# First layer's down projection: later sums, eight block pairs in the last group, blocks from place 2

## The chip, the core and the metric

The kernel runs on one core of one Trainium2 chip. The metric is the device time of one execution in microseconds (us): 2175.49 us is the median of three runs before the change, which lay between 2175.35 and 2177.54 us. One further execution was profiled; all rows below come from it.

## What is computed

The reference is a trunk of two layers over 256 tokens with width 2048. Every layer adds a mixer (attention and a state-space part in the first, dilated attention in the second) and then a gated feed-forward network, and a norm ends the whole:

```python
for layer in range(DEPTH):                       # DEPTH = 2
    hn = rms_norm(h, mix_norm_w[layer])
    mix = even_mixer(hn, ...) if layer % 2 == 0 else odd_mixer(hn, ...)
    h = h + mix
    f = conv_ffn(rms_norm(h, ffn_norm_w[layer]), ..., w_down[layer])
    h = h + f
return rms_norm(h, final_norm_w)

def conv_ffn(hn, w_gate, w_up, conv_w, conv_b, w_down):
    g = causal_dwconv(hn @ w_gate, conv_w, conv_b)
    return (silu(g) * (hn @ w_up)) @ w_down      # the last product: 256 x 5632 by 5632 x 2048
```

The change concerns the last product of the first layer, `@ w_down`, and the first chunks of the odd mixer that follow it.

## The kernel before

**Products in two parts.** All is float32. The kernel splits each operand into a high part (a rounded copy, type fp32r) and a low part (the rest), and multiplies high by high, high by low and low by high: three terms (`TERMS`). A weight chunk arrives by one DMA of 512 KB into a `raw` buffer (four of them); ScalarE (ACT) rounds it to the high part in an `hl` buffer (three of them), L167; VectorE (DVE) subtracts to get the low part, L168. The activations were split before; they are the stationary operand in the down projection, and the weights stream.

**The down projection (`fold`).** It makes four groups of 512 output columns. A group runs over 22 chunks, each a pair of 128-row weight tiles by 512 columns; a chunk is at a place from 0 to 21 in the order `seq`. In group 0 a chunk is multiplied plainly by `whole` (L527, 512 columns each). In groups 1 to 3 a chunk goes one of two ways:

- *flat* (`flat` and `halves`, L575 and L578): the weight split of 1024 columns, then 24 matmuls of 256 columns;
- *block* (`pair_prep` and `seven`, L542): the chunk is seen as a 2 by 2 matrix of blocks and multiplied in the manner of Strassen and Winograd with seven block products instead of eight, 21 matmuls of 256 columns. `pair_prep` needs sums of weight blocks and splits them too: DVE L500, L503, L504 (sums), L505, L508, L509 (low parts), ACT L496, L506, L507 (high parts). The matching sums of the activations are made once, in group 0, by `pair_sums` (`S`), for nine chunks (`SP7`), and are kept in 16 `x` tiles, and in lent corners for the ninth.

Flat chunks stand first, then block and flat in turn: blocks at the odd places 3 to 19, so places 0, 1, 2, 20 and 21 are flat twice or thrice in a row.

**Sums at the end.** Four of the seven block products stay in two PSUM banks of their own (`aux1`) over the whole group. After the last block chunk `gather` turns them into the four column blocks' shares (ACT L611, DVE L612 to L616, "block sums"). After the last chunk `unfold` adds the group's PSUM rows (DVE L622, "row sums"; in group 0 an ACT copy), transposes the result on TensorE (PE, L631), adds it to the residual `h` (DVE L635) and sums squares for the next norm (ACT L637, DVE L638). In the last group the sums lie in a borrowed `raw` buffer, and `scale` makes the split inputs of the next layer: ACT L605, DVE L606, one of each for every one of the 16 tiles of 128 rows. Twelve of these belong to finished groups and four wait for the last group. They write into the `x` tiles that the block sums of the activations held.

**Order.** Helpers that span several chunks are generators in the list `bg`; `tick`, called after each chunk, moves each one on to its next `yield`. The Python order is only a wish: a scheduler puts each engine's instructions into a fixed list, and `issue_after` ties one instruction behind another of the same engine in that list. `self.lo` is the DVE instruction that ends the latest weight split. ACT and DVE work through their lists in order, and so does SyncE (SP), which issues the weight DMAs.

**After the down projection.** `odd` begins with steps of 16 pairs of matmuls (L243) and, after every second step, a plain chunk of values (L527). `token_scale` waits a number of ticks, sums the squares (DVE L123, PE L335), takes the root (small DVE operations) and spreads the result (PE L343, ACT L347 into `rbc`), which is first needed when a head's queries are finished after step 6.

## Time and profile before

| what | value |
|---|---|
| median of three runs | 2175.49 us (2175.35 to 2177.54) |
| the profiled execution | 2174.72 us, its span 2172.9 us, granted TensorE clock 0.999 |
| PE, busy share of the span | 99% (2161.1 us) |
| DVE, busy share | 77% (1681.0 us) |
| ACT, busy share | 57% (1228.0 us) |
| down projection of layer 1: groups 1, 2, 3 begin at | 902.92, 960.79 and 1018.72 us |
| first matmul of the odd mixer | 1080.03 us |

The span is the time from the first to the last profiled instruction; 1.8 us of the execution lie around it. A row of the timeline gives start, duration and engine; when like instructions follow each other they are one row with their count (x24). Matmul durations overlap, so the pace of PE is read from the starts of rows, not from the durations. Behind a row, in square brackets, stands how long the engine had been idle and what released it.

### The profile page before, as it was taken

To read this page: it belongs to the slowest core of one execution; us is meant where nothing else is said; L and a number is where in the kernel's file an instruction comes from. 1 tells how busy PE (TensorE), PEld (TensorE's weight loads), DVE (VectorE), ACT (ScalarE), POOL (GpSimd) and SP (SyncE) were. 2 spreads that over 40 slices of the span, in tenths; PEclk is the share of its full clock that TensorE was granted. 3 is DMA by queue.
4 is the path that set the end of the run, shared out by engine and by line. 5 is a ranking of instruction groups with operands and counts; after the bars stand their busy time and mean duration, and the time that the engine had idled before them with its cause. 6 is when DMAs were issued, how large, how long until landed. Compare 5 with 4: busy or idle time off the path is not lost.

```text
span 2172.9 us, 35607 instructions
## 1 busy us (share of the span) xinstructions
PE 2161.1 (99%) x13720; PEld 1948.9 (90%) x13720; DVE 1681.0 (77%) x2717; ACT 1228.0 (57%) x1857; POOL 96.8 (4%) x107
## 2 busy tenths in 40 slices
PE   9999999999999999999999999999999999999998
PEld 8888888888888888899989999888888888888998
DVE  8788776766666668789889998767676767688997
ACT  7556554655555555555555665546555555555554
POOL 0000000101010100000000000000010101000000
PEclk9999999999999999999999999999999999999999
DMA  7654555556556565556555555555555656566664
GB/s 264 236 171 148 172 184 194 191 193 193 194 193 193 195 193 192 194 194 204 182 188 186 188 169 196 171 190 188 185 194 194 194 194 194 193 201 201 209 202 169
DMA packets 117722, 417.65 MB, mean 192 GB/s; under 512 B 13072, under 2 KB 15408, under 8 KB 117552
## 3 DMA queue, kind: packets, MB, share of 16 engines
q1 hardware_dynamic: 116352, 412.48, 57.9%
q8 instruction: 107, 1.75, 0.3%
q0 software_dynamic: 576, 2.10, 0.3%
q10 hardware_dynamic: 624, 0.81, 0.1%
q14 instruction: 63, 0.52, 0.1%
HBM read 413.22 MB, written 2.11 MB: 191 GB/s over the span
## 4 chain that ended last, share of the span: by engine, by line
PE 96%; DVE 3%; issue 0%; DMA 0%; ACT 0%; DVEq 0%; ACTq 0%
PE acc L243 68%; PE acc L578 8%; PE acc L527 6%; PE aux L542 4%; PE acc L542 4%; PE acc L253 1%; PE aux L527 1%; DVE hl L168 1%; PE acc L204 1%; PE acc L260 1%; PE acc L212 0%; PE aux L212 0%; PE aux L970 0%; PE aux L1002 0%; DVE hl L505 0%
## 5 line engine op out<-in xcount | busy, mean ns | idle before, releaser
L243 PE MATMUL acc<-x,hl 128*128 128x512 f32 (+1 forms) x7680 | 1325.9, 334 | 0.0
L243 PEld LDWEIGHTS acc<-x,hl 128*128 128x128 f32 x7680 | 1158.7, 188 | 149.9 <-issue 0.9
L168 DVE TENSOR_TENSOR hl<-raw,hl 128x1024 fp32r<-128x1024 f32 x686 | 839.4, 1224 | 410.1 <-ACT hl L167 404.2
L167 ACT CAST hl<-raw 128x1024 fp32r<-128x1024 f32 x686 | 720.2, 1050 | 620.1 <-PE acc L243 363.6
L578 PE MATMUL acc<-hl,act 128*128 128x256 f32 x1848 | 223.8, 277 | 2.1 <-DVE hl L168 1.6
L578 PEld LDWEIGHTS acc<-hl,act 128*128 128x128 f32 x1848 | 217.0, 188 | 3.5 <-DVE hl L168 2.3
L243 PE MATMUL acc<-o,hl 128*128 128x512 f32 (+1 forms) x1024 | 176.0, 333 | 0.0
L302 ACT COPY ev<-acc 128x256 f32<-128x256 f32 x242 | 90.0, 372 | 149.5 <-PE acc L243 147.5
L243 PEld LDWEIGHTS acc<-o,hl 128*128 128x128 f32 x1024 | 154.4, 188 | 19.9
L868 POOL TENSOR_TENSOR cv<-cv,rbc 128x256 f32<-128x256 f32 x88 | 93.7, 1083 | 852.7 <-ACT cv L867 852.7
L527 PE MATMUL acc<-hl,act 128*128 128x512 f32 x528 | 120.1, 389 | 0.0
L527 PEld LDWEIGHTS acc<-hl,act 128*128 128x128 f32 x528 | 99.0, 188 | 20.5
L303 DVE TENSOR_TENSOR ev<-acc,ev 128x256 f32<-128x256 f32 x242 | 101.3, 421 | 4.4 <-ACT ev L302 2.7
L506 ACT CAST ts<-tf 128x768 fp32r<-128x768 f32 x78 | 65.2, 836 | 49.1 <-DVE tf L503 48.9
L508 DVE TENSOR_TENSOR ts<-tf,ts 128x768 fp32r<-128x768 f32 x78 | 74.4, 954 | 1.8 <-ACT ts L506 1.8
L500 DVE TENSOR_TENSOR tf<-raw 128x512 f32<-128x512 f32 x78 | 53.9, 691 | 9.6 <-DMA raw<-in_wd 8.0
L496 ACT CAST hl<-raw 128x768 fp32r<-128x768 f32 x54 | 45.1, 835 | 23.6 <-PE acc L578 13.1
L542 PE MATMUL aux<-ts,x 128*128 128x256 f32 x414 | 55.7, 276 | 0.0
L542 PE MATMUL acc<-hl,act 128*128 128x256 f32 x324 | 54.3, 276 | 0.0
L505 DVE TENSOR_TENSOR hl<-raw,hl 128x768 fp32r<-128x768 f32 x54 | 51.5, 954 | 1.9 <-ACT hl L496 1.6
L542 PEld LDWEIGHTS aux<-ts,x 128*128 128x128 f32 x414 | 50.9, 188 | 0.0
L878 DVE TENSOR_TENSOR ev<-ev,cv 128x256 f32<-128x256 f32 x88 | 38.3, 437 | 10.3 <-POOL cv L868 1.6
(280 smaller groups left out, 1693.1 us busy)
## 6 DMA issues: line engine op xcount, KB each, us to landing
raw<-in_wg SPq DMA_DIRECT2D x176, 512.0 KB, 4.1
raw<-in_wu SPq DMA_DIRECT2D x176, 512.0 KB, 4.2
raw<-in_wd SPq DMA_DIRECT2D x176, 512.0 KB, 4.2
raw<-in_wev SPq DMA_DIRECT2D x76, 512.0 KB, 3.8
raw<-in_wod SPq DMA_DIRECT2D x64, 512.0 KB, 3.9
raw<-in_wevo SPq DMA_DIRECT2D x32, 512.0 KB, 3.6
raw<-in_wodv SPq DMA_DIRECT2D x32, 512.0 KB, 3.6
raw<-in_wodo SPq DMA_DIRECT2D x32, 512.0 KB, 3.7
```

The source lines that it names most:

```text
L167: nc.scalar.copy(hi, raw)
L168: self.lo = nc.vector.tensor_tensor(lo, raw, hi.bitcast(F32), ALU.subtract)
L243: self.mm = self.nc.tensor.matmul(accs[nt][:, :n], hl[w][:, k, nt * P : (nt + 1) * P], xs[k0 + k][:, :n], start=start and k == w == 0, sto ...
L302: nc.scalar.copy(t, acc[:, T:])
L303: nc.vector.tensor_tensor(t, acc[:, :T], t, ALU.add)
L500: v.tensor_tensor(two(blk(f123, 0, 2)), two(blk(raw, 1, 2)), blk(raw, 3).unsqueeze(1).broadcast_to([P, 2, T]), ALU.subtract)
L506: nc.scalar.copy(t123[0], f123)
L508: v.tensor_tensor(t123[1], f123, t123[0].bitcast(F32), ALU.subtract)
L527: self.nc.tensor.matmul(row.rearrange("p (j c) -> p j c", c=T), self.part(a[k], p, tt), self.both(hl, w, k), start=start and i == k == 0, ...
L542: self.nc.tensor.matmul(to, x[p], w[b][q], start=n == 0 and i in start, stop=n == 2 and i in stop, skip_group_check=alone or i in m,)
L578: mm(row[:, j * T : (j + 1) * T] if own is None else own[:, :T], x, w[:, j], start=first, stop=stop and k == 1 and i == 2 and j == halves[-1],
L868: nc.gpsimd.tensor_tensor(c, c, self.rbc, ALU.mult)
```

## The change

Four things are altered in `fold`, and one number in `odd`.

1. `gather` and `unfold` begin with a bare `yield`, so that each of their steps is traced one chunk later.
2. Their first additions that read PSUM go through `behind`, which ties them behind the latest weight split in DVE's list.
3. The list `some` names the block chunks of a group: nine in groups 1 and 2, eight in group 3 (the chunk with index 7 is multiplied flat there). Blocks stand at the even places from 2 on: 2 to 18 in groups 1 and 2, 2 to 16 in group 3, and all later places are flat.
4. The twelve `scale` steps of finished groups are traced over the last four chunks, three each, and no longer over the last two, six each.
5. In `odd`, `token_scale` waits five ticks, not two.

```diff
+        def behind(*args):
+            with self.tc.issue_after(self.lo.ins):
+                v.tensor_tensor(*args)
+
         def gather(m, y):
             x = lambda i: y[i // 2][:, i % 2 * T : (i % 2 + 1) * T]
+            yield
             nc.scalar.copy(x(0), m[1])
-            v.tensor_tensor(x(2), m[6], x(0), ALU.add)
+            behind(x(2), m[6], x(0), ALU.add)
             v.tensor_tensor(x(1), x(2), m[5], ALU.subtract)
             yield
-            v.tensor_tensor(x(2), m[7], x(2), ALU.add)
+            behind(x(2), m[7], x(2), ALU.add)
             v.tensor_tensor(x(3), x(2), m[5], ALU.subtract)
 
         def unfold(g, rows, y):
+            yield
             for tt in range(NT):
                 if g:
-                    v.tensor_tensor(y[tt], rows[tt], y[tt], ALU.add)
+                    behind(y[tt], rows[tt], y[tt], ALU.add)
...
             seq = list(range(n))
+            some = []
             if g:
-                nx = iter(range(SP7, n))
-                sx = iter([SP7 - 1, *range(SP7 - 1)] if g == WG - 1 else range(SP7))
-                seq = [next(sx if i % 2 and i > 2 else nx) for i in range(n - 2)] + list(nx)
-            left = SP7 if g else 0
+                some = [SP7 - 1, *range(SP7 - 2)] if g == WG - 1 else list(range(SP7))
+                nx, sx = iter([i for i in seq if i not in some]), iter(some)
+                seq = [next(nx if i < 2 or i % 2 else sx) for i in range(2 * len(some) + 2)] + list(nx)
+            left = len(some)
...
-                if out and ci >= n - 2:
-                    scale(range(6 * (ci - n + 2), 6 * (ci - n + 3)))
+                if out and ci >= n - 4:
+                    scale(range(3 * (ci - n + 4), 3 * (ci - n + 5)))
...
     def odd(self, xs, sums, normw):
-        self.bg.append(self.token_scale(sums, 2, 2))
+        self.bg.append(self.token_scale(sums, 5, 2))
```

What the scheduler makes of it stands at three places. In the rows a name's number tells one buffer from another.

**DVE, from the last block chunk of group 3 on.** Before (`hl1483` is the block chunk of place 19, `hl1504` and `hl1506` are the flat chunks of places 20 and 21, `hl1543` and `hl1548` are the first two steps of `odd`, `raw1502` is the borrowed buffer of the sums):

```order
L509 TENSOR_TENSOR hl1483_10866<-tf1485_10869,hl1483_10866 128x256
L612 TENSOR_TENSOR raw1502_10916<-aux1433_10352,raw1502_10916 128x256
L613 TENSOR_TENSOR raw1502_10916<-raw1502_10916,aux1432_10351 128x256
L615 TENSOR_TENSOR raw1502_10916<-aux1433_10352,raw1502_10916 128x256
L616 TENSOR_TENSOR raw1502_10916<-raw1502_10916,aux1432_10351 128x256
L168 TENSOR_TENSOR hl1504_10921<-raw1503_10920,hl1504_10921 128x1024
L168 TENSOR_TENSOR hl1506_10964<-raw1505_10963,hl1506_10964 128x1024
L168 TENSOR_TENSOR hl1543_11046<-raw1542_11045,hl1543_11046 128x1024
L622 TENSOR_TENSOR raw1502_10916<-acc1422_10248,raw1502_10916 128x512
```

With the change (`hl1475` is the block chunk of place 16, `hl1496` to `hl1504` are places 17 to 21, `hl1541` and `hl1545` the first two steps of `odd`; L611 is the line of `behind`, L619 and L622 are the two subtractions of `gather`):

```order
L509 TENSOR_TENSOR hl1475_10773<-tf1477_10776,hl1475_10773 128x256
L168 TENSOR_TENSOR hl1496_10825<-raw1495_10824,hl1496_10825 128x1024
L611 TENSOR_TENSOR raw1494_10823<-aux1430_10315,raw1494_10823 128x256
L619 TENSOR_TENSOR raw1494_10823<-raw1494_10823,aux1429_10314 128x256
L168 TENSOR_TENSOR hl1498_10857<-raw1497_10856,hl1498_10857 128x1024
L611 TENSOR_TENSOR raw1494_10823<-aux1430_10315,raw1494_10823 128x256
L168 TENSOR_TENSOR hl1500_10894<-raw1499_10893,hl1500_10894 128x1024
L622 TENSOR_TENSOR raw1494_10823<-raw1494_10823,aux1429_10314 128x256
L168 TENSOR_TENSOR hl1502_10929<-raw1501_10928,hl1502_10929 128x1024
L168 TENSOR_TENSOR hl1504_10964<-raw1503_10963,hl1504_10964 128x1024
```

One weight split (place 17) now stands between the last block chunk and the block sums, and the four block sums are spread between splits instead of standing in one piece ahead of them.

**DVE, where group 3 begins.** Before (`hl1428` and `hl1431` are places 1 and 2, `raw1434` and `hl1435` the first block chunk, place 3; L622 are the row sums of group 2):

```order
L500 TENSOR_TENSOR tf1437_10357<-raw1434_10353 128x512
L503 TENSOR_TENSOR tf1437_10357<-raw1434_10353,tf1437_10357 128x256
L168 TENSOR_TENSOR hl1428_10286<-raw1427_10285,hl1428_10286 128x1024
L622 TENSOR_TENSOR y1416_10181<-acc1352_9529,y1416_10181 128x512
L622 TENSOR_TENSOR y1417_10182<-acc1353_9530,y1417_10182 128x512
L504 TENSOR_TENSOR tf1437_10357<-raw1434_10353,tf1437_10357 128x256
L168 TENSOR_TENSOR hl1431_10323<-raw1430_10322,hl1431_10323 128x1024
L508 TENSOR_TENSOR ts1436_10355<-tf1437_10357,ts1436_10355 128x768
```

With the change (`hl1425` and `hl1427` are places 0 and 1, `raw1431` and `hl1432` the first block chunk, now place 2; L611 are the row sums):

```order
L500 TENSOR_TENSOR tf1434_10320<-raw1431_10316 128x512
L503 TENSOR_TENSOR tf1434_10320<-raw1431_10316,tf1434_10320 128x256
L168 TENSOR_TENSOR hl1425_10249<-raw1424_10248,hl1425_10249 128x1024
L504 TENSOR_TENSOR tf1434_10320<-raw1431_10316,tf1434_10320 128x256
L508 TENSOR_TENSOR ts1433_10318<-tf1434_10320,ts1433_10318 128x768
L168 TENSOR_TENSOR hl1427_10278<-raw1426_10277,hl1427_10278 128x1024
L611 TENSOR_TENSOR y1414_10152<-acc1352_9527,y1414_10152 128x512
L611 TENSOR_TENSOR y1415_10153<-acc1353_9528,y1415_10153 128x512
L505 TENSOR_TENSOR hl1432_10317<-raw1431_10316,hl1432_10317 128x768
L509 TENSOR_TENSOR hl1432_10317<-tf1434_10320,hl1432_10317 128x256
```

The row sums still stand behind the split of place 1, and what is now behind them is the rest of the first block chunk and no flat split.

**PE, where `odd` sums the squares.** Before (`hl1562` is step 2, `sum1286` the squares):

```order
L243 MATMUL acc1541_11044<-x1490_10904,hl1562_11164 128x512
L243 MATMUL acc1541_11044<-x1490_10904,hl1562_11164 128x256
L243 MATMUL acc1541_11044<-x1491_10905,hl1562_11164 128x512
L335 MATMUL aux1557_11144<-invd_111,sum1286_8845 128x1 x2
L243 MATMUL acc1541_11044<-x1491_10905,hl1562_11164 128x256
```

With the change (`hl1560` is the second chunk of values, `hl1569` is step 4):

```order
L527 MATMUL aux1548_11096<-hl1560_11180,x1480_10809 128x512
L527 MATMUL aux1548_11096<-hl1560_11180,x1481_10810 128x512
L335 MATMUL aux1564_11208<-invd_111,sum1288_8874 128x1 x2
L243 MATMUL acc1538_11035<-x1486_10815,hl1569_11228 128x512
L243 MATMUL acc1538_11035<-x1486_10815,hl1569_11228 128x256
```

The sum of the squares is asked for after the second chunk of values, no longer within step 2. In PE's list the transposes of the row sums (L631, with the change L638) also move on by about one chunk at each of the four ends of a group.

More of the change, by code (lines that the diff above doesn't have):

```diff
@@ L656, in fold @@
                 two = xs[2 * pair : 2 * pair + 2]
-                if g and pair < SP7:
+                if pair in some:
                     if m is None:
@@ L663, in fold @@
                         rows, m, self.pair_prep(panels[g, pair]), two, S[pair],
-                        (1, 7) if left == SP7 - 1 else (), () if left else (5, 6),
+                        (1, 7) if left == len(some) - 1 else (), () if left else (5, 6),
                     )
```

## The prediction

> **What bounds the kernel now.** I read the page's shares first, then who waited for whom, then the timelines around the down projection of layer 1.
>
> ```profile
> PE 2161.1 (99%) x13720; PEld 1948.9 (90%) x13720; DVE 1681.0 (77%) x2717; ACT 1228.0 (57%) x1857; POOL 96.8 (4%) x107
> PE acc L578 <- DVE hl L168: 1.6, 1, 1.6
> PE aux L335 <- DVE sum L123: 0.7, 1, 0.7
> PE acc L578 <- ACT hl L167: 0.4, 1, 0.4
> ```
>
> PE is the bound, with hardly a wait in 2172.9 us. So a change can win only what PE waits or loses in pace, and must pay for every matmul it adds. Of PE's four largest waits three are here: two on L578, the flat chunks, and one on L335, the sum of squares of `odd`. The next rows (busy time by stage: length, PE, PEld, DVE, ACT, POOL, clock, DMA) show where. The stages are groups 2 and 3:
>
> ```profile
> 960.79:1018.72 57.93, 57.93 (x510) 57.84 (x509) 53.13 (x79) 32.77 (x44) 0.00 (x0) 1.00 0.61 201
> 1018.72:1080.20 61.48, 59.41 (x510) 58.52 (x509) 56.02 (x91) 36.32 (x55) 0.00 (x0) 1.00 0.54 176
> ```
>
> Both have 510 matmuls and the clock is full in both, yet group 3 takes 3.4 us longer. PE's timeline tells at which chunks:
>
> ```profile
> 1055.89 2.88 PE L578 MATMUL acc<-hl,act 128*128 128x256 f32 x24
> 1058.62 0.50 PE L542 MATMUL aux<-hl,act 128*128 128x256 f32 x3
> 1060.99 3.23 PE L578 MATMUL acc<-hl,act 128*128 128x256 f32 x24
> 1064.06 0.50 PE L542 MATMUL aux<-hl,act 128*128 128x256 f32 x3
> 1066.44 3.18 PE L578 MATMUL acc<-hl,act 128*128 128x256 f32 x24
> 1069.45 0.50 PE L542 MATMUL aux<-hl,act 128*128 128x256 f32 x3
> 1071.49 0.50 PE L542 MATMUL acc<-hl,act 128*128 128x256 f32 x3
> 1072.38 0.74 PE L578 MATMUL acc<-hl,act 128*128 128x256 f32 x4 [0.39 <-ACT hl L167]
> 1074.75 5.45 PE L578 MATMUL acc<-hl,act 128*128 128x256 f32 x44 [1.62 <-DVE hl L168]
> 1080.03 2.92 PE L243 MATMUL acc<-x,hl 128*128 128x512 f32 x16
> 1091.94 0.58 PE L335 MATMUL aux<-invd,sum 128*128 128x1 f32 x4 [0.66 <-DVE sum L123]
> ```
>
> Start to start, a flat chunk of 24 matmuls takes 1058.62 - 1055.89 = 2.73 us (0.114 each) and a block chunk of 21 takes 1060.99 - 1058.62 = 2.37. A flat and a block together are 5.10. Against this:
> - place 16: 1064.06 - 1060.99 = 3.07, lost 0.34; place 18: 1069.45 - 1066.44 = 3.01, lost 0.28;
> - places 20 and 21: the block chunk of place 19 ends three matmuls after 1071.49, at 1071.83; up to 1080.03 are 8.20 for 2 x 2.73 = 5.46, lost 2.74;
> - L335: 0.66 idle.
>
> Together 0.62 + 2.74 + 0.66 = 4.02 us. That is all there is to win, 0.18% of the time.
>
> **Where the 2.74 comes from.** DVE and ACT at the end of group 3:
>
> ```profile
> 1068.77 0.42 DVE L509 TENSOR_TENSOR hl<-tf,hl 128x256 fp32r<-128x256 f32 x1
> 1071.77 0.42 DVE L612 TENSOR_TENSOR raw<-aux,raw 128x256 f32<-128x256 f32 x1 [2.58 <-PE aux L542]
> 1072.22 0.42 DVE L613 TENSOR_TENSOR raw<-raw,aux 128x256 f32<-128x256 f32 x1
> 1073.48 3.49 DVE L168 TENSOR_TENSOR hl<-raw,hl 128x1024 fp32r<-128x1024 f32 x3
> 1071.02 0.37 ACT L611 COPY raw<-aux 128x256 f32<-128x256 f32 x1 [3.45 <-PE aux L542]
> 1071.28 3.05 ACT L167 CAST hl<-raw 128x1024 fp32r<-128x1024 f32 x3
> ```
>
> The block sums wait for the last block products, and the casts (ACT) and splits (DVE) of places 20 and 21 stand in the same queues behind them. DVE idles 2.58 us, then does four sums and the first of three splits, ready at about 1073.48 + 1.2 = 1074.7, just where PE goes on (1074.75). At the end of group 2 the same sums came behind the split of place 21, and PE lost nothing:
>
> ```profile
> 1012.18 1.23 DVE L168 TENSOR_TENSOR hl<-raw,hl 128x1024 fp32r<-128x1024 f32 x1 [1.45 <-ACT hl L167]
> 1013.32 0.42 DVE L612 TENSOR_TENSOR y<-aux,y 128x256 f32<-128x256 f32 x1
> ```
>
> **Part 1, sums one chunk later and behind a split; blocks from place 2 (places 20, 21: -2.74).** With the change the split of place 17 stands ahead of the block sums, and two sums ahead of place 18's split. Shifted to the new last block chunk, with its end as zero (1071.83 in the rows): DVE starts the first sum at about 0 (L612 at 1071.77), needs 0.45 each for two sums (1071.77 to 1072.22), then 1.2 for the split of place 18: ready at 2.1. ACT's copy and cast are done before that (1071.28 + 1.05 = 1072.33, 0.5 after zero). PE meanwhile works 2.73 us on place 17. So 0.6 us are to spare and the stall costs nothing; bounds 0 and 2.1 (place 17's split late as well). Place 17 itself: its buffer is free once place 14 is done, 5.1 us before it is due, cast and split need 2.3, and DVE comes to it 0.5 us before the block chunk of 2.37 begins (part 2), so the split of 1.2 ends in time. I take 0. The row sums behind `odd`'s first two splits wait for the end of the group, as L622 did.
>
> One thing speaks against the change: the rows show DVE idle at L612 with three splits behind it that do not pass. [...]
>
> **Part 2, the pace of DVE in the alternating part (places 16, 18: -0.62).** The rows of groups of DVE instructions in group 3, and one block-and-flat period without `scale` (two rows of L509):
>
> ```profile
> L606 DVE SCALAR_TENSOR_TENSOR x<-h,params,x 128x256 fp32r<-128x256 f32 x12 | 5.8, 482 | 0.0
> L454 DVE TENSOR_TENSOR ev<-x 128x256 f32<-128x256 f32 x3 | 1.3, 422 | 0.0
> 1031.02 0.42 DVE L509 TENSOR_TENSOR hl<-tf,hl 128x256 fp32r<-128x256 f32 x1
> 1035.87 0.42 DVE L509 TENSOR_TENSOR hl<-tf,hl 128x256 fp32r<-128x256 f32 x1
> ```
>
> A bare period is 4.85 us of DVE for 5.10 of PE. From 1035.87 to 1068.77 six periods carry the 12 L606 and 3 L454 and take 32.90, 5.48 each: DVE loses 0.38 per period, 2.3 in all, and its lead over PE is used up at place 16. With the change (DVE's list) two L606 and two L454 stand in group 2, behind its last block chunk and before five flat chunks in a row; in group 3 five periods carry 10 L606 and 1 L454. Before, 15 extras added 32.90 - 6 x 4.85 = 3.80, 0.25 each; so now 5 x 4.85 + 11 x 0.25 = 27.0 for 5 x 5.10 = 25.5. DVE loses 1.5 instead of 2.3, the last block chunk is 0.8 better off than it was, and the 0.3 by which it was late becomes 0.5 of lead. Part 2 saves 0.62; bounds 0 and 0.62.
>
> **Part 3, eight pairs in group 3 (+0.36).** One chunk changes from block to flat: 2.73 - 2.37, three matmuls. Nothing hides it on PE. Its lighter DVE work is in part 2.
>
> **Part 4, group ends and starts.** The row sums and what follows them cost what they cost; they now meet the first block chunk at place 2.
>
> ```profile
> L505 DVE TENSOR_TENSOR hl<-raw,hl 128x768 fp32r<-128x768 f32 x9 | 8.6, 955 | 0.0
> L509 DVE TENSOR_TENSOR hl<-tf,hl 128x256 fp32r<-128x256 f32 x9 | 3.8, 423 | 0.0
> L635 DVE TENSOR_TENSOR h<-aux,h 128x512 f32<-128x512 f32 x2 | 1.4, 688 | 0.0
> 1018.72 0.40 PE L575 MATMUL acc<-hl,act 128*128 128x512 f32 x1
> 1019.49 1.28 DVE L622 TENSOR_TENSOR y<-acc,y 128x512 f32<-128x512 f32 x2
> 1021.57 0.60 PE L631 MATMUL aux<-consts,y 128*128 128x128 f32 x4
> ```
>
> The list puts the two row sums ahead of L505 and L509 of place 2. They can start when the old group ends (1018.72 here) and take 1.28; L505 and L509 add 0.96 + 0.42: ready 2.7 after the start. Place 2 begins after places 0 and 1, 1021.57 - 1018.72 = 2.85 and 2.73, so 5.6: 2.9 to spare, and nothing is lost. Without that cover each of three group starts pays up to 1.3. The two adds to `h` and two of squares (L635, and L638 of the same size, 0.69 each) follow over places 3 to 6, 2.8 us against that lead of 2.9, and DVE makes up 0.25 per bare period.
>
> **Part 5, `token_scale` later (-0.66).** L335 moves from step 2 to the end of the second chunk of values, behind these two rows:
>
> ```profile
> 1092.37 3.79 PE L243 MATMUL acc<-x,hl 128*128 128x256 f32 x21
> 1096.00 2.91 PE L527 MATMUL aux<-hl,x 128*128 128x512 f32 x12
> 1098.75 0.40 PE L243 MATMUL acc<-x,hl 128*128 128x512 f32 x1
> ```
>
> From 1092.37 to 1098.75 it is 6.4 us later. The sum it needs comes one chunk later, 2.7 us. So 6.4 - 2.7 - 0.66 = 3.0 us to spare, and the wait goes: -0.66. What follows is late next: L343 stands at the end of step 5, one step and a chunk before the queries need `rbc`, 5.4 us for a copy. Bounds 0 and 0.66.
>
> **Other prices.** DMA issues are equal in number, and the SP list has the same loads. After the stall at 1074.75 PE went slower: 44 matmuls in 5.28 us (to 1080.03), 0.120 each against 0.114, with the clock at 1.00. Why, these rows do not say. Five flat chunks in a row now end group 3: if they all ran at 0.120 they would lose 5 x 24 x 0.006 = 0.7; if none does, nothing, and the 0.25 of the two before is already in the 2.74. I take 0, since the rows show it only behind a stall.
>
> **Sum:** -2.74 - 0.62 - 0.66 + 0.36 = -3.66 us. The profiled execution took 2174.72, so 2171.06; the median of the runs is 0.77 above it, and 2175.49 - 3.66 = 2171.83. I say 2171.8. That is 0.17% faster; about 0.2% (4.35 us) is what a measurement of this kernel can tell from no change, and the runs before lay 2.2 us apart, so "faster" in that sense is missed by 0.7 us.
>
> **The rivals.**
>
> *The wait moves on and does not end (13%).* For it: the strict order of DVE, only 0.6 us of cover at place 18, and a DVE list that is still slower than PE (5.4 to 5.1). Against it: one whole split now stands between. If DVE reaches place 17's split late by the old 0.3 and the sums follow, places 16 to 18 lose 0.62 again and some 0.9 at place 18: the gain is 2.1, time 2173.4.
>
> *The row sums stall the first block chunk (8%).* Three group starts at up to 1.3 each, 3.9: the gain is gone, 2175.7. Against it stand 2.9 us to spare; for it, that 1.3 + 2.8 us of adds now fall among block chunks, where DVE has little to give.
>
> *The borrowed buffer starves the loads, slower (6%).* The sums now take a `raw` buffer before place 17's load and keep it until `odd`'s transposes, some nine chunks, where it was four.
>
> ```profile
> raw<-in_wd SPq DMA_DIRECT2D x176, 512.0 KB, 4.2
> 1079.30 1.05 ACT L167 CAST hl<-raw 128x1024 fp32r<-128x1024 f32 x1 [4.97 <-DMA raw<-in_wod]
> ```
>
> For it: ACT waited 4.97 us for a load in just this stretch. A load holds its buffer for 4.2 (issue to landing), 1.05 (cast) and 1.2 (split), 6.5 us; three buffers give a chunk every 2.2, and PE asks for one every 2.73. It decides from 3 x 2.73 = 8.2 us of holding, 1.7 of queueing more than now. At 10 us each of nine chunks would take 3.33, 0.6 too long: +5.4 against -3.66, 2177.2. Against it: that wait of 4.97 followed the stall, which freed the buffers late.
>
> *More than counted (5%).* Group 2 takes 57.93 us for 13 x 2.73 + 9 x 2.37 = 56.8 of chunks; 1.1 go into transposes and a slower start. If their later place saved a third of that in each of three groups, the gain is 4.8, 2170.7. Nothing in the rows says that it does.
>
> **How the numbers follow.** The forecast has 68%; its own range is 2171.0 to 2172.8, from small stalls of up to 0.7 and the scatter of a median. To leave no more than 2 in 10 out, the range takes in the first rival and the scatter of the runs: 2170.3 to 2175.0. Faster by over 0.2% means below 2171.14: a third of the forecast's share (0.22) and the last rival (0.05), 0.27. Slower by over 0.2% means above 2179.8, more than each rival's price: a starved stretch at 12 us of holding, or two rivals at once, 0.05. The rest, 0.68, lies within 0.2%.
>
> **What would show it.** Right: no idle time of PE at the late flat chunks of group 3 nor at L335; groups 2 and 3 equal in length but for 0.36; ACT's copy and DVE's first sum with short idle times, a split ahead of them. Wrong: PE waiting for L168 at place 16 or 18 (part 2, part 1), for L542's operands at place 2 (part 4), ACT or DVE idle on DMA between places 18 and `odd`'s step 2 (borrowed buffer), or L343 waiting for the root (part 5).

## The result and the profile after

| | before | after |
|---|---|---|
| median of 16 runs each | 2175.34 us (2174.18 to 2177.54) | 2171.32 us (2170.90 to 2172.48) |
| the profiled execution, its span | 2174.72, 2172.9 us | 2172.05, 2170.3 us |
| groups 1, 2, 3 begin at | 902.92, 960.79, 1018.72 | 903.92, 961.82, 1019.73 |
| first product of the odd mixer | 1080.03 | 1077.98 |
| first attention product of the odd mixer | 1118.48 | 1115.61 |

The ratio is 0.9982, with a 95% interval of 0.9975 to 0.9990: 4.0 us, just under the 0.2% that counts as a difference here. 2171.8 was forecast.

From the page of the kernel after, busy time and the chain that ended last:

```profile
PE 2161.2 (100%) x13723; PEld 1949.9 (90%) x13723; DVE 1679.6 (77%) x2712; ACT 1227.5 (57%) x1855; POOL 96.8 (4%) x107
PE 99%; DVE 0%; ACT 0%; issue 0%; DVEq 0%
```

PE has three matmuls more, as Part 3 said, and its only wait left in the list is one of 1.1 us at the program's start. All three rows on L578 and L335 are gone. Groups 2 and 3 after, and the odd mixer up to its first attention product (columns as in the stage rows before):

```profile
961.82:1019.73 57.91, 57.91 (x510) 57.82 (x508) 54.12 (x83) 33.05 (x45) 0.00 (x0) 1.00 0.64 202
1019.73:1077.98 58.25, 58.25 (x512) 58.16 (x511) 52.11 (x81) 34.61 (x50) 0.00 (x0) 1.00 0.61 197
1077.98:1115.61 37.63, 37.63 (x210) 32.62 (x209) 32.68 (x71) 20.33 (x28) 0.00 (x0) 1.00 0.59 186
```

Group 3 went from 61.31 to 58.25 us, -3.06, and differs from group 2 by 0.34, the three matmuls. The odd mixer's stretch went from 38.45 (1118.48 - 1080.03) to 37.63, -0.82. Group 1 has 57.90 for 57.87, group 2 57.91 for 57.93. From the first attention product to the end of the span it is 1054.67 after against 1054.43 before, +0.24. Together, from the start of group 1 on, -3.63 us; the forecast was -3.66. Ahead of group 1, where nothing was edited, the profiled execution after is 1.00 us longer (903.92 to 902.92). The 16 times after lie in two clusters, 2170.90 to 2171.51 and 2172.05 to 2172.48, and the profiled one is of the upper; where most of this 1 us lies is told under the last heading.

TensorE's timeline around the last block chunk (place 16) after:

```profile
1059.28 2.88 PE L578 MATMUL acc<-hl,act 128*128 128x256 f32 x24
1062.00 0.50 PE L542 MATMUL aux<-hl,act 128*128 128x256 f32 x3
1064.04 0.50 PE L542 MATMUL acc<-hl,act 128*128 128x256 f32 x3
1064.38 13.77 PE L578 MATMUL acc<-hl,act 128*128 128x256 f32 x120
1077.98 5.61 PE L243 MATMUL acc<-x,hl 128*128 128x512 f32 x32
1095.40 0.50 PE L335 MATMUL aux<-invd,sum 128*128 128x1 f32 x4
```

Places 17 to 21 are one row: 120 matmuls in 13.60 us (1077.98 - 1064.38), 0.1133 each, with no break; before, waits of 0.39 and 1.62 us cut the flat chunks there. L335 has no bracket any more. VectorE beside it:

```profile
1061.63 0.42 DVE L509 TENSOR_TENSOR hl<-tf,hl 128x256 fp32r<-128x256 f32 x1
1061.96 1.22 DVE L168 TENSOR_TENSOR hl<-raw,hl 128x1024 fp32r<-128x1024 f32 x1
1064.31 0.42 DVE L611 TENSOR_TENSOR raw<-aux,raw 128x256 f32<-128x256 f32 x1 [1.13 <-PE aux L542]
...
1065.11 1.22 DVE L168 TENSOR_TENSOR hl<-raw,hl 128x1024 fp32r<-128x1024 f32 x1
```

VectorE still waits for the last block products, but now 1.13 us and not 2.58, since place 17's split (1061.96) stands ahead of the wait. It then does two sums, the second of them in the row left out, and place 18's split, ready at 1065.11 + 1.22 = 1066.33; place 18 begins at 1064.38 + 2.72 = 1067.10. So 0.77 us are to spare where the prediction had 0.6. The last operation for the last block chunk ends at 1061.63 + 0.42 = 1062.05, and that chunk begins at 1062.00; but L509 makes an operand (`T4` in `seven`) that only the seventh product needs, at 1064.04. The thin margin is that of the flat chunk ahead of it, place 15: its split ends at 1059.17 (row under point 2 below) and it begins at 1059.28, 0.11 us later.

### The profile page after: what moved, and what is told of

Same layout as the page of the kernel before. It is cut to its first block, busy times and chain, and to the rows that moved or that the text cites. A ratio compares the mean times of both kernels' runs of the same rounds, so it can differ in the third digit from the quotient of the medians.

```text
span 2170.3 us, 35606 instructions
## 1 busy us (share of the span) xinstructions
PE 2161.2 (100%) x13723; PEld 1949.9 (90%) x13723; DVE 1679.6 (77%) x2712; ACT 1227.5 (57%) x1855; POOL 96.8 (4%) x107
## 4 chain that ended last, share of the span: by engine, by line
PE 99%; DVE 0%; ACT 0%; issue 0%; DVEq 0%
PE acc L243 68%; PE acc L578 10%; PE acc L527 6%; PE aux L542 4%; PE acc L542 4%; PE acc L253 1%; PE aux L527 1%; PE acc L204 1%; PE acc L260 1%; PE acc L212 0%; PE aux L212 0%; PE aux L978 0%; PE aux L1010 0%; PE aux L1000 0%; PE aux L1310 0%; PE aux L177 0%
## 5 line engine op out<-in xcount | busy, mean ns | idle before, releaser
L168 DVE TENSOR_TENSOR hl<-raw,hl 128x1024 fp32r<-128x1024 f32 x687 | 840.9, 1224 | 409.9 <-ACT hl L167 404.1
L578 PE MATMUL acc<-hl,act 128*128 128x256 f32 x1872 | 223.7, 277 | 0.0
L578 PEld LDWEIGHTS acc<-hl,act 128*128 128x128 f32 x1872 | 218.5, 188 | 0.6
L508 DVE TENSOR_TENSOR ts<-tf,ts 128x768 fp32r<-128x768 f32 x77 | 73.4, 953 | 2.2 <-ACT ts L506 2.2
L505 DVE TENSOR_TENSOR hl<-raw,hl 128x768 fp32r<-128x768 f32 x53 | 50.6, 954 | 2.8 <-ACT hl L496 2.5
```

The costliest lines, as they stand in the source:

```text
L168: self.lo = nc.vector.tensor_tensor(lo, raw, hi.bitcast(F32), ALU.subtract)
L508: v.tensor_tensor(t123[1], f123, t123[0].bitcast(F32), ALU.subtract)
L578: mm(row[:, j * T : (j + 1) * T] if own is None else own[:, :T], x, w[:, j], start=first, stop=stop and k == 1 and i == 2 and j == halves[-1],
```

## The experiments

Lengths of the last group are from its first product to the first of the odd mixer. Both kernels are the yardstick: 61.31 before, 58.25 after. Where no times are given, a kernel was executed once, under the profiler, and only its stretches are compared: the start of group 1, ahead of which their edits change nothing, lies anywhere from 902.56 to 905.70 us in them.

**1. Neither the delay nor the tie.** The rest of the change stays.

```diff
         def gather(m, y):
-            yield
...
-            behind(x(2), m[6], x(0), ALU.add)
+            v.tensor_tensor(x(2), m[6], x(0), ALU.add)
```

(and the same for the other `yield` and the other two sums)

> The changed kernel, but the block and row sums are queued as before: without the extra chunk of delay and without the tie to a weight split. Everything else of the change stays (eight pairs in the last group, blocks from place 2, three scalings per chunk, the later token scale). On VectorE the four block sums now stand ahead of place 17's split. Theory (head of the line: the sums wait for the last block chunk's aux products and hold the split that is queued behind them): in the changed kernel the first sum could start 0.27 us after the block chunk ended (1064.31 against TensorE's 1064.04-1064.38), two sums and the split's share take 0.80 us and a split 1.22, so place 17's split ends at about 1064.31 + 1.6 + 1.2 = 1067.1 where place 17 is due at 1064.38: TensorE loses about 2.8 us there and the last group takes 58.25 + 2.8 = 61.0 us (first product of the group to first product of the next layer), the whole run about 2174. Rival (VectorE's load was the cause: with fewer pairs and spread scalings the sums do no harm where they stand): no wait over 0.3 us at place 17, group 58.2 to 58.5 us, run 2171 to 2172.

The group, its products and VectorE's rows at place 17 of this kernel:

```profile
1021.50:1083.05 61.55, 59.51 (x512) 58.62 (x511) 52.49 (x81) 34.47 (x50) 0.00 (x0) 1.00 0.59 186
```

```profile
1061.46 3.18 PE L578 MATMUL acc<-hl,act 128*128 128x256 f32 x24
...
1067.41 0.74 PE L578 MATMUL acc<-hl,act 128*128 128x256 f32 x4 [0.39 <-ACT hl L167]
1069.78 2.44 PE L578 MATMUL acc<-hl,act 128*128 128x256 f32 x19 [1.62 <-DVE hl L168]
```

```profile
1066.79 0.42 DVE L610 TENSOR_TENSOR raw<-aux,raw 128x256 f32<-128x256 f32 x1 [2.58 <-PE aux L542]
1068.50 3.49 DVE L168 TENSOR_TENSOR hl<-raw,hl 128x1024 fp32r<-128x1024 f32 x3
```

61.55 us: the whole gain of the group is gone, and a little more. The waits are those of the kernel before, to the hundredth: VectorE 2.58 at the first sum, TensorE 0.39 for ACT's cast and 1.62 for the split, with eight pairs, another place and spread scalings all in. So where the sums stand in the lists decides, and VectorE's load does not. The rival is out. That gap is 2.6 us of the 3.30; two flat chunks ahead of block chunks (places 13 and 15, the row with 3.18 is one, 2.88 without a wait) lost 0.30 each besides and place 11 0.1, which was not expected (point 2 below).

**2. The ties without the delay.** Two sums stand ahead of place 17's split, two behind it.

> The changed kernel with the ties to a weight split, but without the extra chunk of delay. On VectorE two of the four block sums stand ahead of place 17's split and two behind it. Theory (head of the line): place 17's split ends at about 1064.31 + 0.8 + 1.2 = 1066.3 of the changed kernel's clock, due at 1064.38: a loss of about 2.0 us, the last group 60.2 us. Rival 1 (only the delay by a chunk counts, a tie does nothing): the same loss as without both, 2.8 us, group 61.0. Rival 2 (VectorE's load was the cause): no loss, group 58.2 to 58.5.

The group of this kernel and its products at place 17:

```profile
1018.38:1078.86 60.48, 59.36 (x513) 58.48 (x511) 52.28 (x81) 34.47 (x50) 0.00 (x0) 1.00 0.59 189
```

```profile
1064.15 0.74 PE L578 MATMUL acc<-hl,act 128*128 128x256 f32 x4 [0.39 <-ACT hl L167]
1065.60 6.62 PE L578 MATMUL acc<-hl,act 128*128 128x256 f32 x56 [0.71 <-DVE hl L168]
```

60.48, +2.23 where 2.0 was expected at place 17. That is close by luck: 1.66 of it lie behind the last block chunk (2.59 in the run before) and 0.57 in the flat chunks of places 13 and 15. The wait for the split shrank from 1.62 to 0.71 by two sums of 0.45 each, so every sum in front of the split costs its own time; both rivals gave another number.

Most of what stays is ScalarE's. Its copy of the block sums waits for the block product (3.45 us before the change), and the cast of place 17 stands behind it: in this run the copy starts at 1062.78 and the casts at 1063.05, as they do before the change at 1071.02 and 1071.28 (in the prediction's rows). With 1.05 us for a cast, the split of place 17, due at 1063.60, could not have begun before 1064.1, and it began at 1064.33. So without any sum in front of it some 1.4 us would still be lost, an estimate from these rows. The delay moves the copy behind that cast as well, the tie moves only VectorE's sums; that is why the tie alone brings only a part.

**3. The delay without the ties**, run twice.

> The changed kernel with the extra chunk of delay, but without the ties. On VectorE the order is: place 17's split, all four block sums, place 18's split. Theory (head of the line): place 18's split ends at about 1064.31 + 1.6 + 1.2 = 1067.1 of the changed kernel's clock, and place 18 is due at 1064.38 + 2.72 = 1067.10: a loss of 0 to 0.3 us, the last group 58.25 to 58.55 us; so most of the gain is the delay, and the ties only keep a margin of 0.8 us. Rival (the ties carry the gain: the sums' place relative to every split counts): a loss of 1 us or more at place 18, group over 59.2.

> The delay without the ties, a second time, with more times. In its first profile the last group took 59.01 us, 0.76 more than the changed kernel, with no wait of TensorE at place 18: a gap of 0.04 us at place 16, and from there to the end of the group every 256-column product at 117.8 ns instead of 113.3. Theory A (the pace is drawn anew at such a gap, by chance): the times fall into clusters, and the last group of this profile takes either 58.25 to 58.3 or about 59.0. Theory B (without the ties the gap is always there, and the slow pace follows each time): 59.0 again, and a median some 0.8 us over the changed kernel's 2171.3.

The last group of the first and of the second profile, and a window of the second:

```profile
1018.63:1077.64 59.01, 59.01 (x512) 58.92 (x511) 52.60 (x82) 34.49 (x50) 0.00 (x0) 1.00 0.61 195
```

```profile
1018.65:1078.14 59.49, 59.49 (x512) 59.43 (x511) 53.67 (x84) 34.85 (x51) 0.00 (x0) 1.00 0.61 193
1030.00:1056.00 26.00, 26.00 (x223) 26.00 (x223) 25.93 (x45) 17.82 (x30) 0.00 (x0) 1.00 0.58 189
```

No wait at place 18 in either, so the delay by itself ends the stall, as the theory had it. But the group is 0.76 and 1.24 us longer than the changed kernel's, with TensorE busy throughout. The window shows how: 26.00 us for 223 matmuls are 0.1166 each (the bounds cut a matmul); start to start it is 117.8 ns up to 1060 and 113.3 from there on. In the first profile it was the other way round, 113.3 up to 1058 and 117.8 to the end. So the pace changes at another point each time, which is what theory A of the second run rests on; but 59.49 is neither of its two values nor that of theory B, and the ten times show no clusters. These times, 2171.14 to 2172.37 with a median of 2171.89 in 10 runs, ratio 0.9982 (0.9973 to 0.9991), can't be told from the changed kernel's, and the ties' worth is below what the times can show.

**4. The token scale early again.**

```diff
-        self.bg.append(self.token_scale(sums, 5, 2))
+        self.bg.append(self.token_scale(sums, 2, 2))
```

> The changed kernel with the token scale queued two steps after the layer's start instead of five. Theory: its first product (a ones product over the sums of squares) then stands behind 24 of the 32 products of a chunk, due at about 1086.97 + 24 x 0.171 = 1091.1 of the changed kernel's clock, while VectorE's last sum of squares ends at 1092.0: TensorE waits about 0.9 us there, and the stretch from the odd layer's first product to its first attention product is 37.63 + 0.9 = 38.5 us; the last group stays at 58.25. Rival (the 0.82 us saved there came with the rest of the change, the row sums that end earlier, and not with the later step): no wait over 0.2 us, stretch 37.6 to 37.8.

The odd mixer's stretch in this kernel, VectorE's last sum of squares, and TensorE around L335:

```profile
1077.05:1115.11 38.06, 37.94 (x211) 32.54 (x210) 32.25 (x71) 20.36 (x28) 0.00 (x0) 1.00 0.60 185
```

```profile
1090.04 0.42 DVE L123 TENSOR_TENSOR sum<-sum 128x256 f32<-128x256 f32 x1
```

```profile
1086.04 4.45 PE L243 MATMUL acc<-x,hl 128*128 128x512 f32 x24
1090.61 0.58 PE L335 MATMUL aux<-invd,sum 128*128 128x1 f32 x4
```

The stretch takes 38.06, +0.43 and not +0.9. L335 is due at about 1090.3 and starts at 1090.61 when the sum is done (1090.04 + 0.42 = 1090.46): 0.3 us, and L335 and L343 themselves take 0.07 us longer each than after (0.44 and 0.43 to the next product, for 0.37 and 0.36). Here the sum ends 1.54 us earlier than after (1091.58 + 0.42 = 1092.00 in the row quoted below), and only 0.93 of that is the layer's earlier start, so 0.6 of the wait that was expected is not there. So neither expectation holds: the later step is worth about half of the 0.82 in this one profile, and the other half came with the rest of the change.

**5. Nine pairs in the last group**, with the delay and the ties; run twice.

```diff
-                some = [SP7 - 1, *range(SP7 - 2)] if g == WG - 1 else list(range(SP7))
+                some = [SP7 - 1, *range(SP7 - 1)] if g == WG - 1 else list(range(SP7))
```

> The changed kernel with nine pairs in the last group's block chunks, as before, and the sums still delayed and tied. All 12 scalings and 3 pair sums stand on VectorE within the last group again. Theory (VectorE's pace is a cost of its own): TensorE has three products fewer, -0.36 us, but VectorE is 0.38 us per period behind again and TensorE waits 0.3 to 0.7 us in all at the flat or block chunks of places 16 to 19; the last group takes 58.2 to 58.6 us against the changed kernel's 58.25, so eight pairs gain nothing or a little. Rival (the waits at places 16 and 18 came with where the sums stood, not with VectorE's load): no such wait, last group 57.9 us.

> Nine pairs in the last group with the sums delayed and tied, a second time, with more times. Its first run was 2170.26, below each of the 16 of the changed kernel (2170.9 to 2172.5), although its last group took the same 58.25 us. Theory A (the difference is in the pace of stretches that the edit does not touch, between 81 and 119 us and between 1150 and 1200, by chance): the median of the runs is 2171 to 2172 and the ratio to the kernel before that of the changed kernel, 0.998. Theory B (nine pairs are faster somewhere): a median of 2170.5 or less, below the changed kernel's lower cluster.

The group in the first and in the second profile, with the one chunk of the first that waits:

```profile
1018.37:1076.62 58.25, 58.21 (x510) 57.92 (x508) 55.27 (x91) 36.13 (x54) 0.00 (x0) 1.00 0.61 192
```

```profile
1063.03 3.22 PE L578 MATMUL acc<-hl,act 128*128 128x256 f32 x24
```

```profile
1018.71:1076.62 57.91, 57.91 (x509) 57.82 (x508) 54.19 (x90) 36.13 (x54) 0.00 (x0) 1.00 0.62 191
```

58.25 with one wait of 0.3 us (3.22 against the 2.88 of such a row without a wait), and 57.91 with none. The first is what the theory of the first run gave, the second what its rival gave. So nine pairs cost VectorE its margin but not 0.62 us; they lose nothing or gain 0.34 against the changed kernel's group. In time: 2171.46 in 11 runs (2170.29 to 2172.40), ratio 0.9980 (0.9971 to 0.9989), against 0.9982 (0.9975 to 0.9990). They are one and the same to these measurements, as theory A of the second run had it; neither version is shown to beat the other.

**6. Blocks from place 3 again**, with eight pairs, the delay and the ties.

```diff
-                seq = [next(nx if i < 2 or i % 2 else sx) for i in range(2 * len(some) + 2)] + list(nx)
+                seq = [next(sx if i % 2 and i > 2 else nx) for i in range(2 * len(some) + 2)] + list(nx)
```

> The changed kernel with the block chunks from place 3 on, as before, in all three groups; the sums stay delayed and tied. Theory (the start at place 2 is neither a cost nor a gain: 2.9 us were to spare there): groups 1 and 2 take 57.9 us as in both kernels, the last group 58.25, its end still with four flat chunks, enough for the sums. Rival 1 (the row sums need the early start: with blocks one place later the sums meet the next group's splits): groups 1 and 2 longer by 0.5 us or more. Rival 2 (the early start costs something that is hidden in the 57.9): groups 1 and 2 shorter by 0.3 or more.

The group of this kernel, and two of its three flat chunks that wait:

```profile
1019.62:1078.75 59.13, 59.09 (x513) 58.43 (x511) 53.28 (x83) 35.08 (x51) 0.00 (x0) 1.00 0.59 186
```

```profile
1051.71 3.14 PE L578 MATMUL acc<-hl,act 128*128 128x256 f32 x24
...
1062.47 3.18 PE L578 MATMUL acc<-hl,act 128*128 128x256 f32 x24
```

Groups 1 and 2 stay at 57.92, as expected, but the last group takes 0.88 more: three flat chunks wait 0.26 to 0.30 each. In this kernel all four adds to `h` and to the sums of squares, 2.8 us, fall between the first block chunk's last split and the second's (L509 at 1025.51 and 1032.75): 7.24 us, for 5.20 of TensorE. After, the same stretch is 6.06 (1022.68 to 1028.74), for 5.74 of TensorE, because four transposes fall there too, and two of the adds go to the next period. By the third block chunk little is left of that difference: L509 is done 1.22 us ahead of the chunk here and 1.41 after. What differs from there on is VectorE's list: here the split of a flat chunk stands behind L503 of the next block chunk, and after it stands ahead of it (point 2 below). So the start at place 2 is neither cost nor neutral: undoing it loses 0.88 us in the last group, as these rows read by the list that the scheduler makes with it more than by the adds; no run separates the two.

**7. Nine pairs, with the scalings' low parts on GpSimd.** An attempt to keep the 0.34 and VectorE's margin.

```diff
+                    f = self.ev.tile([P, T], F32, tag="ev", name=self.nm("ev"))
+                    nc.gpsimd.tensor_scalar(f, h, w, None, ALU.mult)
+                    nc.gpsimd.tensor_tensor(x[:, T:], f, x[:, :T].bitcast(F32), ALU.subtract)
-                    v.scalar_tensor_tensor(x[:, T:], h, w, x[:, :T].bitcast(F32), ALU.mult, ALU.subtract)
```

(for the twelve scalings within the last group)

> The changed kernel with nine pairs in the last group, and the 12 low parts that the scalings of that group make moved from VectorE (one operation each) to GpSimd, which has no work there (a product with the norm weight, then a subtraction, at an estimated 1.08 us each, from the 1083 ns of its other 128x256 operations). Theory (VectorE's load sets places 16 to 19): VectorE keeps its lead, no wait of TensorE, the last group takes 58.25 - 0.36 = 57.9 us. Rival 1 (GpSimd's reads and writes slow VectorE, or the low parts come late for the next layer): VectorE's 128x1024 splits take clearly more than 1.22 us, or the next layer's first stretch more than 37.6; then 58.2 us or more. Rival 2 (where the sums stand is all that counts): as nine pairs alone, with no difference between the two kernels.

The group, and VectorE's groups of instructions while GpSimd worked beside it (1034 to 1066), then the same lines after (1034 to 1062):

```profile
1019.26:1082.84 63.58, 59.53 (x509) 58.45 (x508) 58.55 (x77) 35.53 (x54) 23.07 (x21) 1.00 0.56 175
```

```profile
L505 DVE TENSOR_TENSOR hl<-raw,hl 128x768 fp32r<-128x768 f32 x5 | 6.9, 1387 | 0.0
L168 DVE TENSOR_TENSOR hl<-raw,hl 128x1024 fp32r<-128x1024 f32 x5 | 6.1, 1215 | 0.0
L503 DVE TENSOR_TENSOR tf<-raw,tf 128x256 f32<-128x256 f32 x5 | 4.3, 861 | 0.2
```

```profile
L168 DVE TENSOR_TENSOR hl<-raw,hl 128x1024 fp32r<-128x1024 f32 x6 | 7.3, 1223 | 0.0
L505 DVE TENSOR_TENSOR hl<-raw,hl 128x768 fp32r<-128x768 f32 x5 | 4.8, 956 | 0.0
L503 DVE TENSOR_TENSOR tf<-raw,tf 128x256 f32<-128x256 f32 x5 | 2.1, 425 | 0.0
```

63.58 us, 5.33 more than after. Rival 1, by other rows than it named: the 128x1024 splits kept their 1.22 us and the next layer's first stretch its 37.6, but L505 went from 956 to 1387 ns on average and L503 from 425 to 861, a period of VectorE takes 6.08 us for 5.10 of TensorE, and TensorE waits at five flat chunks. (In this list the split of a flat chunk also stands behind L503 and L504.) L168 (1215 ns, 1223 after) and L508 (0.95 us in both kernels) did not become longer; by what way GpSimd's work lengthens some and not others, these rows do not say. Moving work off a busy engine to an idle one cost more here than it freed.

**8. What sets TensorE's pace: the offset of the weights.** First the first chunk of groups 1 to 3 at the offset of the others:

```diff
-                    hl = self.flat(panels[g, pair], 0 if g == 0 else OFF if ci else OFF - 8)
+                    hl = self.flat(panels[g, pair], 0 if g == 0 else OFF)
```

> The changed kernel, where the first flat chunk of groups 1 to 3 keeps its split weights 8 columns further on in its buffer, where the other flat chunks have them; nothing else. It asks what sets TensorE's pace: 256-column products start every 113.3 ns nearly everywhere, but every 118 ns in places 0 and 1 of each group, with a granted clock of 1.00. Theory A (the offset of the weights in their buffer sets it): places 0 and 1 run at 113.3 too, each group some 0.35 us shorter: 57.5 and 57.5 and 57.9 us. Theory B (it is a state that a break in the stream of products starts, whatever the addresses): places 0 and 1 stay at 117 to 118 and the groups at 57.9, 57.9, 58.25 us, but for a chance change of pace elsewhere.

This kernel was executed once. Its groups 1 and 3:

```profile
904.45:964.22 59.77, 59.77 (x509) 59.68 (x507) 50.82 (x75) 32.69 (x44) 0.00 (x0) 1.00 0.62 192
...
1023.99:1084.11 60.12, 60.12 (x513) 60.04 (x512) 51.79 (x81) 34.50 (x50) 0.00 (x0) 1.00 0.61 189
```

Both theories fail, and the answer is larger than either: all three groups are 1.87 us longer, at 118 ns from end to end, without a wait and at a clock of 1.00. One chunk at another offset sets the pace of the 21 behind it. Then the other projections:

```diff
-            hl = self.prep(panel[od[ci]], apart=kind == self.chan)
+            hl = self.prep(panel[od[ci]], apart=kind == self.chan, off=OFF if ci else OFF - 8)
```

and the same with `OFF - 8` for every chunk.

> The changed kernel, where the projections whose weights are held as two separate halves or as interleaved pairs (the stretch from 40 to 133 us of the first layer, and those of the second layer) keep the first chunk of each panel 8 columns further forward in its buffer. It follows up the run with the first chunk of the groups at the common offset: there every group then ran at 118 ns per 256-column product from end to end, so the offset of one chunk sets the pace of what comes behind it. In the stretch from 51 to 120 us the changed kernel ran at 118 in its profile, and the kernel before only from 81 to 119. Theory A (a chunk at another offset brings the fast pace back): 113 in most of 40 to 133 us, up to 2.5 us shorter, time about 2169 to 2170. Theory B (the offset acts only together with block chunks, or the pace is drawn anew at breaks): the pace of that stretch as in one of the other profiles, time 2171 to 2172.5, no difference that the rounds can tell.

> As the run before, but all chunks of those projections lie 8 columns further forward, not only the first of each panel. Theory A (a change of offset between neighbouring chunks matters, not the offset itself): as the changed kernel, 2171 to 2172.5, 118 ns over most of 51 to 120 us. Theory B (the offset itself sets the pace): one pace throughout these projections, either 113 (time 2169 to 2170) or 118 (time over 2173).

From 300 to 850 us, with the first chunk moved, then with all moved, then the kernel after:

```profile
300.00:850.00 550.00, 550.00 (x3155) 482.39 (x3155) 377.60 (x559) 292.65 (x434) 45.53 (x45) 1.00 0.60 188
```

```profile
300.00:850.00 550.00, 550.00 (x3178) 484.51 (x3177) 380.70 (x566) 295.92 (x439) 45.57 (x45) 1.00 0.61 190
```

```profile
300.00:850.00 550.00, 550.00 (x3231) 486.82 (x3230) 386.99 (x580) 301.94 (x447) 47.75 (x47) 1.00 0.60 194
```

2201.03 us (ratio to the kernel before 1.0117, 1.0102 to 1.0132) and 2194.95 (1.0088, 1.0071 to 1.0105). No chunk brought the quick pace back; they took it away. With the first chunk moved that is neither theory, with all moved it is theory B: one pace throughout, 118 ns, and a time over 2173. In the same 550 us TensorE does 76 and 53 matmuls fewer, so a pair of 512 and 256 columns takes 0.3487, 0.3461 and 0.3405 us (twice 550 over the count). From start to start in the traces, the matmuls after are 226 to 227 and 113 to 114 ns apart. With all moved they are 228 and 118 apart, and 98% of the pairs take 0.346 to 0.348 us. With the first of a panel moved, the 512-column ones change between 228, 232 and 233 ns, and no stretch of it is at the quick pace.

## Why the prediction was right, point by point

The stretches from group 1 on give -3.63 us for the forecast -3.66, and the median is 0.5 us below the forecast one. That the first two agree to 0.03 is luck in part: group 3 gave 0.06 more than its three terms (-3.06 for -3.00), the odd mixer 0.16 more, and 0.25 that was not forecast was lost elsewhere.

**1. The block sums (-2.74): right, and shown.** Undoing the delay and the tie brings the old waits back exactly (2.58, 0.39, 1.62); half of it brings a part. The margin at place 18 was put at 0.6 and is 0.77. Of the two devices the delay does the work; the ties move two sums behind another split. One reading of the step is not borne out: that the three splits behind L612 "do not pass". No split was ready in those 2.58 us. The first one's cast stood in ScalarE's list behind the copy that waited 3.45 us, began at 1071.28 and could end at 1072.33, 0.5 us after place 20 was due (1071.83). So the rows do not show whether VectorE would let a ready split pass a sum that waits. What they show of the order is this: the cast was held, since its load had landed at 1067.0 (issued at 1063.49, 3.5 us to landing) and its buffer was free once place 17 had ended (1066.44); and the split, ready by 1072.33, began at 1073.48, behind two sums that began at 1072.68 and 1073.14. The step named both lists and then put the whole 2.74 to VectorE's; by the estimate from the run with the ties alone, some 1.4 us of it would stay for ScalarE's copy.

**2. VectorE's pace (-0.62): the size is right, its cause was not.** The step put it on the eight pairs, as "DVE loses 1.5 instead of 2.3", and held the start at place 2 for neutral ("the row sums and what follows them cost what they cost"). The waits at places 16 and 18 did go. But undoing eight pairs brought back 0.3 in one profile and nothing in the other, undoing the start at place 2 brought back 0.86 at three flat chunks, and undoing the delay brought back 0.57 at two flat chunks.

The loss per period came as forecast: the five periods behind the third block chunk (L509 from 1034.67 to 1061.63) took 26.96 us, and 27.0 were forecast. The lead at their start did not: it was 1.41 us (1035.09 to 1036.50), where before it was 1.92 (1036.29 to 1038.21). So at the last block chunk the lead is -0.05, where 0.5 was forecast. What the step does not have is the place of the flat chunk's split. After (place 15) and before (place 18), the split and the sum of the next block chunk that is nearest to it:

```profile
1057.95 1.22 DVE L168 TENSOR_TENSOR hl<-raw,hl 128x1024 fp32r<-128x1024 f32 x1
1059.09 0.42 DVE L503 TENSOR_TENSOR tf<-raw,tf 128x256 f32<-128x256 f32 x1
```

```profile
1064.83 0.42 DVE L503 TENSOR_TENSOR tf<-raw,tf 128x256 f32<-128x256 f32 x1
1065.56 1.22 DVE L168 TENSOR_TENSOR hl<-raw,hl 128x1024 fp32r<-128x1024 f32 x1
```

After, the split stands ahead of L503 and is done 0.11 us before place 15 begins (1059.17 and 1059.28). Before, it stands behind L503 and is done 0.34 us after place 18 begins (1066.78 and 1066.44). L503 takes 0.42 us, so with the old order place 15 would be some 0.3 late, the size of each wait that went. The scheduler has the split behind L503 again in the runs with neither, with the ties alone and with blocks from place 3, and in these, flat chunks wait, most of them 0.26 to 0.31; with the delay alone and with the early token scale it stands ahead, and no flat chunk loses more than 0.04. With nine pairs it stands ahead too, and one flat chunk waits in one of two profiles. So the order in the list goes with the waits but for that one; no run moves the split alone, so that it is the cause is argued, not shown.

**3. Eight pairs (+0.36): right in size.** 58.25 against 57.91 for nine without a wait. With point 2 this part of the change brings nothing, or takes 0.34.

**4. Group ends and starts (0): right for groups 1 and 2, wrong for group 3.** These rows of the kernel after, VectorE's last for place 2 and TensorE's first product of place 2:

```profile
1022.68 0.42 DVE L509 TENSOR_TENSOR hl<-tf,hl 128x256 fp32r<-128x256 f32 x1
```

```profile
1025.66 0.60 PE L542 MATMUL aux<-hl,act 128*128 128x256 f32 x3
```

Place 2 is ready at 1023.10 and due at 1025.66, 2.6 to spare for the 2.9 forecast, so no group start pays for the row sums, and groups 1 and 2 kept their length. In group 3 the start at place 2 is a gain, told in experiment 6 and point 2.

**5. The token scale (-0.66): right in sign, mis-sized.** The stretch gave 0.82, of which 0.43 is the later step by itself, in one profile. The spare time was put at 3.0 and is 3.4:

```profile
1091.58 0.42 DVE L123 TENSOR_TENSOR sum<-sum 128x256 f32<-128x256 f32 x1
```

(done at 1092.00, L335 at 1095.40).

**The other price, 0.120 us against 0.114 behind a stall ("why, these rows do not say").** Taken as 0, and it was 0 in places 17 to 21, 0.1133 each. In the first profile of the experiment without ties it was 0.76. The step called it something that shows "only behind a stall"; the runs show it without one. From start to start in the trace, the 44 matmuls behind the stall before are mostly 117 to 119 ns apart: the slower pace of the last section.

**The rivals.** The wait did not move on, but by little (0.11 us at place 15 and 0.77 at place 18). The row sums stalled no block chunk. The borrowed buffer cost nothing: ScalarE does wait for the loads of places 20 and 21, 1.33 and 1.55 us, the sign that was named for it, but PE waits for none. More was not counted: groups 1 and 2 are the same to 0.03.

## What to carry to other kernels

ScalarE's instructions ran here in the order of its list: before the change a cast whose load had landed at 1067.0 began at 1071.28, behind a copy that waited 3.45 us. So ask what stands behind an instruction that waits, and ask it of every engine on the way: moving a copy of ScalarE and four sums of VectorE behind one cast and one split was worth 2.6 us of the bound engine, with no work saved. The lead of the feeding engine was a store for the whole stage (1.41 us at the third block chunk, -0.05 at the last), so an edit that looks free at its own place is to be judged at the end of the stage, and by the list that the scheduler made of it: one operation of 0.42 us in front of a split, or behind it, goes here with flat chunks that wait 0.3 us or not at all. And before a difference of 1 us in 2170 is put down to an edit, compare the stretches that the edit does not touch, here by counting matmuls in equal windows.

## What was not expected of the hardware

**TensorE has more than one pace at a full clock.** Matmuls of 256 columns start every 113.3 ns or every 117.8, those of 512 every 227, 228 or 232 to 233, and the granted clock is 1.00 in all. A pace can last for hundreds of matmuls: after, nearly all of the 3231 from 300 to 850 us take 113 to 114 or 226 to 227 ns from start to start, and the 196 from 84 to 118 us take 117 or 233. In the runs of experiment 8 it went with the place of the weights in their buffer: 8 columns (32 bytes) on one chunk in 22 cost 1.87 us per group, and the same on one chunk in each panel of the other projections some 29 us in all (2201.03 against 2175.74 for the kernel before in the same rounds, and the change's 4 on top). And in some stretches it changes from one execution to the next, with the same instructions. The stretch from 52 to 80 us, before and then after:

```profile
52.00:80.00 28.00, 28.00 (x167) 24.86 (x166) 22.33 (x46) 15.38 (x23) 0.00 (x0) 1.00 0.67 214
```

```profile
52.00:80.00 28.00, 28.00 (x162) 24.50 (x161) 22.12 (x45) 15.07 (x23) 0.00 (x0) 1.00 0.66 208
```

Five matmuls fewer in this window are most of the 1.0 us by which the profiled execution after is longer ahead of group 1 (a pair of 512 and 256 columns takes 0.34 us, so 2.5 pairs are 0.9). The kernel without ties has 161 there in its first profile and 167 in its second, the same instructions. From 84 to 118 us it has 201 in its first profile and 196 in its second, as the changed kernel has, so this stretch moves by 0.9 us as well. The two clusters of times after are most likely such stretches at one pace or the other; that is argued from these profiles, since the changed kernel itself was profiled once. What sets the pace there, and whether the break of 0.04 us that the first profile without ties has where its slow pace begins has to do with it, stays open.

**GpSimd beside VectorE** made L503, a 128x256 sum, take twice as long (861 ns against 425), while the 128x1024 splits took the same 1.22 us. In the trace GpSimd does nothing beside most of such a split (from 1049.85 to 1051.46; the split runs from 1049.59 to 1050.80), and beside one that it does meet its product takes 2.03 us for 0.98 (from 1036.73; the split from 1036.84). So the one split ran mostly alone, and beside the other it was GpSimd's product that took longer.
